# First tile projected without its shift, the shift's share added in PSUM, and later panels given a new split

## The chip, the cores and the metric

The kernel runs on one core of one Trainium2 chip. The metric is the device time of one execution in microseconds. Before the change the median of three runs is 1839.45 us (1839.06 to 1840.63).

A core has five engines that run their own instruction queues beside each other and wait for one another through semaphores: TensorE (PE) for matmuls, VectorE (DVE), ScalarE (ACT), GpSimd (POOL), and SyncE (SP), which here issues the transfers between device memory and the core's own memories. PE writes its results to PSUM, of which this kernel holds eight buffers (banks) of up to 128 x 512 fp32 numbers; DVE and ACT read them from there.

## The reference

Two layers over a sequence of 2048 frames of width 1024, each a normalised, conditioned input, a mixer and a gated residual, and a last normalisation:

```python
c_act = jax.nn.silu(c)
for i in range(DEPTH):
    cond = c_act @ ada_w[i] + ada_b[i]
    shift = cond[:, None, :D_MODEL]
    scale = cond[:, None, D_MODEL:2 * D_MODEL]
    gate = cond[:, None, 2 * D_MODEL:]
    h = rmsnorm(x, norm_g[i]) * (1.0 + scale) + shift
    ...
    x = x + gate * out
return rmsnorm(x, final_g)
```

Layer 0 is a recurrent block: `h @ in_w` gives 2 x 1024 columns, one half through a causal convolution of four taps, two gates and a linear recurrence over time, the other half as a SiLU gate, then an output projection. Layer 1 is a gated delta rule with eight heads of 128: `h @ in_w` gives q, k, v and z, 4 x 1024 columns, and 16 more columns, from which each head's decay and beta come. Everything is fp32.

What matters for the change: the projection of the first layer is `(x_norm * scale + shift) @ W`, which equals `(x_norm * scale) @ W + shift @ W`. The second term is one row, the same for all frames.

## The kernel before, in words

**Products.** An fp32 product of a weight panel (1024 x 128) and a tile of 512 frames is made of three reduced products (fp32r): both operands are split into a high and a low part, and high x high, high x low and low x high are summed in one PSUM bank. For each of 8 k-steps of 128 that makes three matmuls, 24 for a panel and a tile (`products`, line 721, matmul in line 728). Panels are loaded by `panel_load` (655) and split by `panels_thread` (665): `whi` on ACT (704), `wlo` on DVE (710). `keep_thread` (715) stores the low half for the second unit of frames.

**Order of work.** The program is written by a planner (`Weave`, lines 78 to 174) when it is built. Each thread is a generator; a `yield` names an event, a buffer slot, or an engine with the time that the step is thought to take there, and the planner picks the step that can start first (priority settles ties). This fixes the order of each engine's queue; on the chip only semaphores decide when things run. Durations of the steps off PE are scattered by one per cent by a random generator, so that its seeds choose among orders; before, `w.count()` sets a new seed of `SEEDS` every 16 jobs (88 to 91).

**Stages.** Layer 0 takes its frames in two units of 1024, each of two tiles of 512 (`in1`), with 16 panels, x and z in turn, then the output projection `out1`; layer 1 the same with 32 panels (`in2`), the heads beside it, and `out2`. A job is one panel and one tile (`job`, 731); `project_thread` (760) runs the jobs in the order of `plans` (639 to 651): in the first unit panels 0 and 1 over both tiles, these four jobs side by side, then the others one by one, each over both tiles.

**The start.** What must arrive is: the first tile of x, 2 MB (`norm_thread`, 526), the first panels, and the conditioning weights of layer 0, 4 MB each for scale and for shift, in four quarters of two k-steps (`first_loads_thread`, 330). SP issues x, panel 0, quarter 0 of scale and shift in turns, panel 1, quarters 1 and 2, the second tile of x, quarter 3. PE computes scale with four matmuls of 32 output columns side by side, each writing its own 32 partitions of one bank, called column groups here (396), sums these with `corner` (326, called from 403), and DVE finishes the columns (316, 319). DVE sums shift itself (422), and PE turns that into columns (427). Idle matmuls on the identity stand before and in between (380; `BEFORE`, `BEHIND`, line 38). The tile of x is scaled by its row norm (516), transposed by PE (550), and `split_thread` (614) makes `h = tile * scale + shift` on ACT (620), its high half on ACT or DVE (625, 628) and its low half on DVE (630). A k-step's products wait for that k-step's split.

**After a job.** `conv1_thread` convolves an x panel from PSUM (805 to 832, DVE line 819) and frees the bank; `z1_thread` makes the gate (846, 848). `gates_thread` makes the two gates (861), the recurrence (890) and the output. The banks: tags `mm`, `d`, `c` and `tp`, two each. The second unit's tiles are turned through device memory: `turned_thread` (575), scaled (516), transposed on DVE (563), stored, loaded again (`reload_thread`, 600) and split.

**The decay columns.** `decay_thread` (1062), once a unit, loads the 1024 x 16 weights, splits them into high and low side by side (32 columns), and for each tile runs 16 matmuls of 512 frames (1085) once all k-steps of the tile are split; then ACT copies, PE folds and turns (1096), and a chain on DVE and ACT makes decay and beta, on which all heads of the unit wait.

Of the kernel before, what the change touches and what calls it, by code (L numbers as in the profile page):

```python
# [17 lines left out]
P = 128  # L18
# [7 lines left out]
NH = 8  # L26
# [3 lines left out]
TP = 5  # L30
TURN = 2
# [6 lines left out]
BEFORE, BEHIND = (0, 3, 5, 0, 0, 0, 0, 0), (4, 0, 0, 0)  # L38
# [4 lines left out]
SEEDS, SPREAD = (32, 45, 51, 36, 4, 54, 53, 16, 3, 25, 36, 8, 28, 14, 37, 0, 0), 0.01  # L43
# [34 lines left out]
class Weave:  # L78
    def __init__(self):
        self.free = dict.fromkeys(("pe", "act", "dve", "pool", "sp", "dma"), 0.0)  # L80
        self.held = {"dve2": [], "pool2": []}
        self.table = "exp"
        self.landed, self.through = [0.0] * 8, 0.0
        self.scatter, self.jobs = random.Random(SEEDS[0]), 0
        self.threads = []
        self.now = 0.0

    def count(self):
        self.jobs += 1
        if self.jobs % 16 == 0:  # L90
            self.scatter = random.Random(SEEDS[self.jobs // 16])
# [86 lines left out]
def trunk_kernel(ctx, tc, x, head, small, ada0, ada_w, ada_b, final_g, w1, gate_w, ow1, w2, wab, ow2, out):  # L178
# [20 lines left out]
    def flat(ap):  # L199
# [13 lines left out]
    fold = cp.tile([32, 32], F32, name="fold")  # L213
    pool.memset(fold, 0.0)
    pool.tensor_tensor(fold[:, 0:16], ident[0:32, 0:16], ident[0:32, 16:32], ALU.add)

    corner = cp.tile([P, 1], F32, name="corner")
    dve.tensor_reduce(out=corner, in_=ident.rearrange("p (m c) -> p m c", c=32)[:, :, 0], axis=mybir.AxisListType.X,
                      op=ALU.add)

    small_s = cp.tile([P, SMALL], F32, name="small_s")

    def part_of(tile_in, at, *shape):
# [10 lines left out]
    cond = cp.tile([P, 2, 2, KT], F32, name="cond")  # L234
    sp2 = cp.tile([P, KT], F32, name="sp2")
# [11 lines left out]
    tags |= {t: ("l1", n) for t, n in {"xf1": 3, "tg": 4, "th": 2, "tz": 2, "gw": 2, "head": 1}.items()}  # L247
# [3 lines left out]
        "xe": 2, "xf": 2, "kt": KTN, "qt": QTN, "vt": 1, "ec": 4, "eca": 3, "gr": 1, "middle": 1, "ac": 4, "kd": 5, "vn": 4,  # L251
        "rq": 4, "nk": 4, "oo": 2, "tblk": 1, "ttmp": 1, "tf": 1, "zt": 2, "t2": 2, "yt": 2, "so": 2, "ro": 2,
        "ssk": 2, "ssq": 2, "rk": 2, "cc": 2, "junk": 1, "ab": 1, "gin": 1, "gg": 1, "spe": 1, "spd": 1, "beta": 2,
        "gs": 2, "eg": 2}.items()}

    for t in ("xe", "xf", "vt", "eca", "gr", "middle", "ab", "gin", "gg", "spe", "spd"):
        tags[t] = ("l2a", tags[t][1])
# [70 lines left out]
    H = TC // 2  # L328

    def first_loads_thread():  # L330

        yield ev("firstpanel")
        for q in range(4):
            if q == 1:
                yield ev("firstpanels")
            if q == 3:
                yield ev("loaded", (("in1", 0), 1))
            if q % 2 == 0:
                p = hp if q == 0 else pools["hc"]
                raws = [p.tile([P, KT, TC], F32, tag=f"h{'lh'[part]}{'BC'[q // 2]}", name=f"ada{part}{q}") for part in range(2)]  # L340
                raws = [flat(r).rearrange("p (a k c) -> p a k c", a=2, c=H) for r in raws]
            for part in range(2):
                w.set(ev("adaraw", part, q), raws[part][:, q % 2])
            for g in range(2):
                for part in (1, 0):
                    yield "sp", 1.3, False
                    sp.dma_start(out=raws[part][:, q % 2, 4 * g:4 * g + 4, :], in_=ada0[4 * part + q, :, 4 * g:4 * g + 4, :])
                    w.spawn(arrive_thread(ev("adaload", part, q, g)), 0)
            w.set(ev("adaissue", q))
# [28 lines left out]
    def idle_products(pt, n):  # L378
        for _ in range(n):
            pe.matmul(pt[:, 3 * P:4 * P], lhsT=ident, rhs=ident, start=True, stop=True)  # L380

    def first_pe_thread():

        rest = ps.tile([P, TC], F32, tag="mm", name="rest")
        idle_products(rest, 42)
        c_bc, ttok = yield ev("cbc")
        for q in range(4):
            raw = yield ev("adaraw", 1, q)
            ctok = yield slots["c"]
            pt = ps.tile([P, TC], F32, tag="c", name="adaps")  # L390
            for g in range(2):
                yield ev("adaload", 1, q, g)
                yield "pe", 1.15 if q + g else 2.2, 0.0 if g == 0 else 0.2
                idle_products(pt if g == 0 else rest, BEFORE[2 * q + g])
                for j in range(4):
                    pe.matmul(pt[32 * j:32 * j + 32, 0:H], lhsT=c_bc[:, 4 * g + j, :], rhs=raw[:, 4 * g + j, :],
# [4 lines left out]
            act.copy(tmp, pt[:, 0:H])  # L401
# [7 lines left out]
    def first_dve_thread():  # L409

        yield ev("c")
        for q in range(4):
# [10 lines left out]
            ctok = yield slots["c"]  # L423
            yield "pe", 0.5
            pt = ps.tile([P, TC], F32, tag="c", name="adac")
            idle_products(pt, BEHIND[q])
            columns_of(acc, pt, 2, ones[:, 0:1])
            put("tz", ttok)
            yield from finish_columns(0, 0, 2 * q, 2, pt[:, 0:2])
            put("c", ctok)  # L430
        yield ev("cond", 0, 1, KT - 1)
        w.set(ev("ada"))

# [92 lines left out]
    def norm_thread(key, layer, src, t0, slot, before, after, xtags=("b4",) * TB, htag="hf"):  # L526
# [17 lines left out]
        for k in range(KT):  # L544
            bank = "d" if slot == "A" and k % 2 else "tp"
# [29 lines left out]
    def turned_thread(key, layer, src, t0, slot, before, between, after):  # L575
# [16 lines left out]
        w.spawn(reload_thread(key, t_d), TP)  # L592
# [3 lines left out]
        for k in range(KT):  # L596
            xk, hold = yield ev("xk", key, k // 2)
            w.spawn(split_thread(layer, xk[:, k % 2, :], hold.done, hh, hl, k, ev("split", key, k), "hf"), 1)

    def reload_thread(key, t_d):  # L600
        for k in range(KT // 2):
# [4 lines left out]
            w.spawn(arrive_thread(ev("xk", key, k), (xk, Hold(w, slots["b4"], tok, 2))), 0)  # L606
# [6 lines left out]

    def split_thread(layer, pt, release_, hh, hl, k, done, tag, first=False):
        for part in (1, 0):
# [4 lines left out]
        act.activation(h, pt, AF.Identity, bias=cond[:, layer, 0, k:k + 1], scale=cond[:, layer, 1, k:k + 1])  # L620
# [1206 lines left out]
```

## Time and profile before

| | |
|---|---|
| median of 3 runs | 1839.45 us |
| the profiled execution | 1837.33 us |
| its span, first to last instruction | 1835.3 us |
| DVE busy | 1344.3 us |
| ACT busy | 1137.4 us |
| bytes moved | 322.76 MB, mean 176 GB/s |

The profile is of one execution. Its page gives busy time and share for each engine, the span in 40 slices, the DMA queues, the chain of work that ended last (followed back from the last instruction: at each step to what released it, or to the instruction before it on its engine), and the costliest groups of instructions. Further views used below: windows (busy time of each engine in a stretch), the order of time (start, length, engine, line, operation, output <- inputs, shapes, count, and in brackets idle time before and what ended it), the chain of waits in order of time, and groups by line. An fp32 matmul leaves two records (`x2`), an fp32r matmul one. Lengths of PE's records overlap, since matmuls are pipelined; the step from one to the next is shorter than the length.

### The profile page before, as it was taken

What the parts mean: (1) busy time and instruction counts of PE and PEld (TensorE: products, weight loads), DVE (VectorE), ACT (ScalarE), POOL (GpSimd) and SP (SyncE); (2) the same over time, 40 slices, a digit from 0 to 9 for tenths busy, and PEclk for the clock granted to TensorE, in tenths of its full rate; (3) what the DMA queues carried; (4) which work ended last, traced back from release to release, by engine and by line L of the source; (5) the groups of instructions that cost most, each with busy time, mean ns of one, the idle gap of its engine ahead of it and who ended that gap; (6) DMA issues with size and microseconds to landing.
All of it is one profiled execution on the core that took longest, in us unless ns stands there. A gap on an engine that the chain in (4) does not pass through costs nothing.

```text
span 1835.3 us, 31223 instructions
## 1 busy us (share of the span) xinstructions
PE 1806.3 (98%) x10378; PEld 1454.5 (79%) x10378; DVE 1344.3 (73%) x3113; ACT 1137.4 (62%) x2683; POOL 363.8 (20%) x895
## 2 busy tenths in 40 slices
PE   8999999999999999999999999999999999999998
PEld 7777777777877878787888788787888887878887
DVE  7989878777545647878788887677766786876653
ACT  5766777666112357687877676776787687664221
POOL 2111001000001014223333231231223132211100
PEclk9999999999999999999999999999999999999999
DMA  9567755555578735667677666456655556686741
GB/s 361 145 199 206 238 165 192 177 165 173 191 207 228 226 104 147 162 162 186 162 186 174 144 159 214 121 153 154 151 137 141 149 149 140 167 261 180 244 146 69
DMA packets 510425, 322.76 MB, mean 176 GB/s; under 512 B 369844, under 2 KB 437940, under 8 KB 510264
## 3 DMA queue, kind: packets, MB, share of 16 engines
q1 hardware_dynamic: 510264, 320.77, 62.7%
q8 instruction: 82, 1.34, 0.3%
q14 instruction: 79, 0.65, 0.1%
HBM read 219.93 MB, written 100.73 MB: 175 GB/s over the span
## 4 chain that ended last, share of the span: by engine, by line
PE 72%; DVE 10%; DMA 7%; ACT 5%; issue 2%; SPq 2%; POOL 1%; DVEq 0%; POOLq 0%; ACTq 0%
PE mm L728 41%; PE mmo L728 16%; PE pg L861 3%; DVE xf L781 2%; DMA raw<-in_w 1%; PE py L1454 1%; DVE tblk L1322 1%; PE pS L1467 1%; PE pS L1466 1%; PE pp L1437 1%; DVE ttmp L1319 1%; PE pp L1438 1%; PE pqk L1287 1%; PE pkk L1199 1%; DMA yf<-y_d 1%
## 5 line engine op out<-in xcount | busy, mean ns | idle before, releaser
L781 DVE SCALAR_TENSOR_TENSOR xf<-xe,small_s,xf 128x512 f32<-128x512 f32 x288 | 215.7, 753 | 49.8 <-ACT xf L1040 46.0
L704 ACT CAST whi<-raw 128x1024 fp32r<-128x1024 f32 x96 | 100.0, 1042 | 25.8 <-DMA raw<-in_w 20.6
L1319 DVE TENSOR_TENSOR ttmp<-blk,tblk 128x60 f32<-128x60 f32 (+24 forms) x496 | 104.7, 211 | 14.6 <-DMA blk<-blk_d 2.4
L1322 DVE TENSOR_TENSOR tblk<-tblk,ttmp 128x60 f32<-128x60 f32 (+24 forms) x496 | 105.7, 213 | 12.7 <-DVE ttmp L1319 0.3
L728 PE MATMUL mm<-hh_('in2', 1)_11643,whi 128*128 128x512 f32 x256 | 104.4, 408 | 0.6 <-ACT xe L793 0.5
L728 PE MATMUL mm<-hh_('in2', 1)_11918,whi 128*128 128x512 f32 x256 | 104.0, 406 | 0.7 <-ACT tz L1055 0.7
L728 PE MATMUL mm<-hl_('in2', 1)_11919,whi 128*128 128x512 f32 x256 | 104.0, 406 | 0.0
L728 PE MATMUL mm<-hh_('in2', 1)_11643,wlo 128*128 128x512 f32 x256 | 103.8, 405 | 0.0
L728 PE MATMUL mm<-hh_('in2', 0)_5199,whi 128*128 128x512 f32 x256 | 103.6, 405 | 0.0
L728 PE MATMUL mm<-hh_('in2', 1)_11918,wlo 128*128 128x512 f32 x256 | 103.5, 404 | 0.0
L728 PE MATMUL mm<-hl_('in2', 1)_11644,whi 128*128 128x512 f32 x256 | 103.5, 404 | 0.0
L728 PE MATMUL mm<-hh_('in2', 0)_5088,wlo 128*128 128x512 f32 x256 | 103.4, 404 | 0.0
L728 PE MATMUL mm<-hh_('in2', 0)_5088,whi 128*128 128x512 f32 x256 | 103.3, 404 | 0.0
L728 PE MATMUL mm<-hh_('in2', 0)_5199,wlo 128*128 128x512 f32 x256 | 103.2, 403 | 0.0
L728 PE MATMUL mmo<-oh,oh 128*128 128x512 f32 (+1 forms) x264 | 103.1, 390 | 0.0
L728 PE MATMUL mm<-hl_('in2', 0)_5200,whi 128*128 128x512 f32 x256 | 102.9, 402 | 0.0
L728 PE MATMUL mm<-hl_('in2', 0)_5089,whi 128*128 128x512 f32 x256 | 102.8, 402 | 0.0
L728 PE MATMUL mmo<-ol,oh 128*128 128x512 f32 (+1 forms) x264 | 102.5, 388 | 0.0
L728 PE MATMUL mmo<-oh,ol 128*128 128x512 f32 (+1 forms) x264 | 102.4, 388 | 0.0
L728 PE MATMUL mmo<-oh,yl 128*128 128x512 f32 x256 | 101.0, 395 | 1.1 <-DVE yl L971 1.1
L728 PE MATMUL mmo<-oh,yh 128*128 128x512 f32 x256 | 101.0, 395 | 0.4 <-ACT yh L967 0.4
L728 PE MATMUL mmo<-ol,yh 128*128 128x512 f32 x256 | 100.8, 394 | 0.0
(325 smaller groups left out, 5315.8 us busy)
## 6 DMA issues: line engine op xcount, KB each, us to landing
raw<-in_w SPq DMA_DIRECT2D x96, 512.0 KB, 4.1
araw<-in_ada_w SPq DMA_DIRECT2D x32, 512.0 KB, 4.7
xt<-x_d SPq DMA_DIRECT2D x32, 512.0 KB, 5.4
xt_d<-xb SPq DMA_DIRECT2D x192, 64.0 KB, 2.7
xk<-xt_d SPq DMA_DIRECT2D x24, 512.0 KB, 6.2
xt<-in_x SPq DMA_DIRECT2D x16, 512.0 KB, 6.3
ada<-in_ada SPq DMA_DIRECT2D x16, 512.0 KB, 10.9
y_d<-tz SPq DMA_DIRECT2D x32, 256.0 KB, 3.3
```

The lines of the kernel that those rows point to most:

```text
L704: act.copy(hi, raw)
L728: pe.matmul(pt, lhsT=lhs[a][:, k, :], rhs=rhs[b][:, k, :], start=(k == 0 and n == 0), stop=(k == KT - 1 and n == 2))
L781: dve.scalar_tensor_tensor(xf, xe[:, 1 + j:1 + j + TC], wc[:, j:j + 1], xf, ALU.mult, ALU.add)
L861: pe.matmul(pg, lhsT=gw[:, g, :], rhs=xf, start=True, stop=True)
L1199: pe.matmul(pkk[:, b, :], lhsT=kc, rhs=kc, start=True, stop=True)
L1287: pe.matmul(pqk[:, b, :], lhsT=kt[:, b * P:(b + 1) * P], rhs=qt[:, b * P:(b + 1) * P], start=True, stop=True)
L1319: dve.tensor_tensor(tmp, blk[:, j, j + 1:32].unsqueeze(2).to_broadcast([P, r, c_]), t[:, j, 0:c_].unsqueeze(1).to_broadcast([P, r, c_]), A ...
L1322: dve.tensor_tensor(t[:, j + 1:32, 0:c_], t[:, j + 1:32, 0:c_], tmp, ALU.subtract)
L1437: pe.matmul(pp[:, 0, :], lhsT=kc, rhs=S_, start=True, stop=True)
L1438: pe.matmul(pp[:, 1, :], lhsT=qc, rhs=S_, start=True, stop=True)
L1454: pe.matmul(py, lhsT=rm[:, b, :], rhs=zt, start=True, stop=True)
L1466: pe.matmul(pS[:, 0, :], lhsT=kd[:, b, :], rhs=yt, start=True, stop=True)
```

## The change

1. **Conditioning.** `first_loads_thread` loads all of scale, then all of shift; `first_panels_thread` loads four panels, one behind the first x tile and the others each behind a quarter of scale. The idle products between are gone.
2. **First tile without shift.** `split_thread` applies only the scale to the first tile. Jobs 0 to 3 are panels 0 to 3 on the first tile, jobs 4 to 7 the same panels on the second; all eight are spawned together. Panels 2 and 3 are split into buffers (`yh`, `yl`) that are used only later otherwise.
3. **The shift's share.** `bias_thread` multiplies the four panels with the shift as soon as that is there (16 matmuls for a panel, four column groups, fp32), splits the result, and two more products per panel add it to the bank through `comb`, in which each column sums the four groups.
4. **New split.** After jobs 0 to 3, `shift_thread` adds the shift to the first tile, k-step by k-step, and splits it again; from the fifth panel on jobs wait for that.
5. **Second tile.** Its x is loaded behind all of the shift, into the buffers of the first tile.
6. **Decay columns.** `ab_thread` runs them in fp32, four k-steps side by side in the four column groups, on h before its split; the weights are loaded once. In layer 1 `split_over_thread` makes h in place.
7. **Order.** One seed; `TP` 5 to 4, `TURN` 2 to 3 (transposed blocks in flight), three `tz` buffers for two.

```diff
-TP = 5
-TURN = 2
+TP = 4
+TURN = 3
...
-BEFORE, BEHIND = (0, 3, 5, 0, 0, 0, 0, 0), (4, 0, 0, 0)
...
-SEEDS, SPREAD = (32, 45, 51, 36, 4, 54, 53, 16, 3, 25, 36, 8, 28, 14, 37, 0, 0), 0.01
+SEED, SPREAD = 4, 0.01
...
+    FIRST = 4
...
     def first_loads_thread():
         yield ev("firstpanel")
...
+        for part in (1, 0):
...
+            for q in range(4):
+                w.set(ev("adaraw", part, q), raws[q // 2][:, q % 2])
+                for g in range(2):
+                    yield "sp", 1.3, False
+                    sp.dma_start(out=raws[q // 2][:, q % 2, 4 * g:4 * g + 4, :], in_=ada0[4 * part + q, :, 4 * g:4 * g + 4, :])
+                    w.spawn(arrive_thread(ev("adaload", part, q, g)), 0)
+                w.set(ev("adaissue", part, q))
+                if part and q == 0:
+                    yield ev("panelissue", q + 1)
+
+    def first_panels_thread():
+        name, panels, _ = plans[0]
+        yield ev("small")
+        yield ev("loaded", (("in1", 0), 0))
+        for m in range(FIRST):
+            if m:
+                yield ev("adaissue", 1, m - 1)
+            got = yield from panel_load(name, panels[m])
...
+    def bias_thread():
+        name, panels, jobs = plans[0]
+        ctok = yield slots["hf"]
+        yield ev("c")
+        yield "dve", 0.6
+        comb = tile_([P, TC], "hf", "comb", F32R)
+        dve.tensor_copy(out=comb, in_=corner.to_broadcast([P, TC]))
+        for k in range(KT):
+            yield ev("cond", 0, 0, k)
...
+        for n in range(FIRST):
+            halves = (yield ev("w", name, panels[n]))[0:2]
+            btok = yield slots["c"]
...
+            pt = ps.tile([P, P], F32, tag="c", name="pbias")
+            yield "pe", 0.55, 0.0
             for g in range(2):
...
+                for a in range(2):
+                    for j in range(4):
+                        pe.matmul(pt[32 * j:32 * j + 32], lhsT=sh[:, 4 * g + j, :], rhs=f(halves[a])[:, 4 * g + j, :],
+                                  start=(g + a == 0), stop=(g + a == 2))
+            yield "act", 0.3
+            act.copy(both[:, n % 2, 0, :], pt)
+            yield "dve", 0.25
+            dve.tensor_tensor(both[:, n % 2, 1, :], pt, f(both[:, n % 2, 0, :]), ALU.subtract)
...
+        for n in range(FIRST):
+            yield ev("job", name, n)
...
+            w.spawn(shift_thread(key, hh, hl, k), 2)
+
+    def shift_thread(key, hh, hl, k):
+        ttok = yield slots["hf"]
+        yield "act", 0.711
+        t = tile_([P, TC], "hf", "hs")
+        act.activation(t, f(hh[:, k, :]), AF.Identity, bias=cond[:, 0, 0, k:k + 1], scale=1.0)
+        yield "dve2", 0.599
+        dve.tensor_tensor(t, t, f(hl[:, k, :]), ALU.add)
+        yield "act", 0.524
+        act.copy(hh[:, k, :], t)
+        yield "dve2", 0.599
+        dve.tensor_tensor(hl[:, k, :], t, f(hh[:, k, :]), ALU.subtract)
...
     def split_thread(layer, pt, release_, hh, hl, k, done, tag, first=False):
-        for part in (1, 0):
+        for part in (1,) if first else (1, 0):
             yield ev("cond", layer, part, k)
...
+        if first:
+            act.activation(h, pt, AF.Copy, scale=cond[:, layer, 1, k:k + 1])
...
+        if u == 0:
+            jobs = [(p, i) for i in range(NTC) for p in panels[:FIRST]] + [(p, i) for p in panels[FIRST:-2] for i in range(NTC)] + pair(*panels[-2:])
...
     def job(name, jobs, n):
...
+        yield from products(pt, (hi, lo), h, (lambda k: ev("shifted" if first and n >= FIRST else "split", (name, i), k)),
+                            more=first and n < FIRST)
+        if first and n < FIRST:
+            comb, both = yield ev("bias", n)
+            for a in range(2):
+                yield "pe", MM, 0.0
+                pe.matmul(pt, lhsT=both[:, a, :], rhs=comb, start=False, stop=(a == 1))
...
+    def ab_thread(u):
+        yield ev("wab")
         for i in range(NTC):
...
+            for g in range(0, KT, 4):
+                hs = []
+                for k in range(g, g + 4):
+                    hs.append((yield ev("h", (("in2", u), i), k)))
...
+                yield "pe", 0.87, 0.0 if g == 0 else 0.2
+                for k in range(4):
+                    pe.matmul(pab[32 * k:32 * k + 32], lhsT=wab_s[:, 16 * (g + k):16 * (g + k) + 32], rhs=hs[k][0], start=(g == 0), stop=(g > 0))
...
-        w.spawn(norm_thread((in1[0], 1), 0, x, TC, "B", [ev("adaissue", 2)], [ev("cond", 0, 1, 3), ev("cond", 0, 0, 3)],
-                            ("yh", "yh", "yl", "yl"), "tg"), 2)
+        w.spawn(norm_thread((in1[0], 1), 0, x, TC, "B", [ev("adaissue", 0, 3)], [ev("cond", 0, 1, KT - 1)], htag="tg"), 2)
```

More of the change, by code (lines that the diff above doesn't have):

```diff
@@ L422, in first_dve_thread, with shift_columns_thread @@
                     dve.scalar_tensor_tensor(acc, raw[:, k], c_col[:, k:k + 1], acc, ALU.mult, ALU.add)
[L423 to L430, printed above, removed]
+            w.spawn(shift_columns_thread(q, acc, ttok), 0)
+        for k in range(KT):
+            yield ev("cond", 0, 0, k)
         yield ev("cond", 0, 1, KT - 1)
         w.set(ev("ada"))
+    def shift_columns_thread(q, acc, ttok):
+        ctok = yield slots["c"]
+        yield "pe", 0.4
+        pt = ps.tile([P, 2], F32, tag="c", name="adac")
+        columns_of(acc, pt, 2, ones[:, 0:1])
+        put("tz", ttok)
+        yield from finish_columns(0, 0, 2 * q, 2, pt)
+        put("c", ctok)
     def columns_thread():
@@ L544, in norm_thread @@
         for k in range(KT):
-            bank = "d" if slot == "A" and k % 2 else "tp"
+            bank = "tp"
             ptok = yield slots[bank]
@@ L741, in job @@
         bank = ("d" if layer == 1 else "c") if kind in "vz" else "mm"
-        if name == ("in1", 0) and n < 4:
-            bank = "mm" if n < 2 else "d"
+        first = name == ("in1", 0) and i == 0
         mtok = yield slots[bank]
         pt = ps.tile([P, TC], F32, tag=bank, name="mm")
-        yield from products(pt, (hi, lo), h, (lambda k: ev("split", (name, i), k)))
+        yield from products(pt, (hi, lo), h, (lambda k: ev("shifted" if first and n >= FIRST else "split", (name, i), k)),
[5 more added lines that the diff above has]
+                pe.matmul(pt, lhsT=both[:, a, :], rhs=comb, start=False, stop=(a == 1))
         if all(q != p for q, _ in jobs[n + 1:]):
-            put("whi", htok)
-            put("wlo", ltok)
+            put(*htok)
+            put(*ltok)
         if layer == 1:
@@ L765, in project_thread @@
             for n in range(len(jobs)):
-                w.count()
-                if name == ("in1", 0) and n < 4:
+                if name == ("in1", 0) and n < 2 * FIRST:
                     w.spawn(job(name, jobs, n), 8 + n)
-                    if n == 3:
-                        for m in range(4):
+                    if n == 2 * FIRST - 1:
+                        for m in range(2 * FIRST):
                             yield ev("job", name, m)
@@ L1747, in trunk_kernel @@
         w.spawn(xr_thread(), 3)
+        w.spawn(wab_thread(), 3)
+        for u in range(NU):
+            w.spawn(ab_thread(u), 2)
         w.spawn(phase1_end_thread(), 0)
```

195 lines of the change are left out of this document (104 added, 91 removed).

## The prediction

> **What bounds the kernel now.** I read the page first: the busy shares and the chain of work that ended last.
>
> ```profile
> PE 1806.3 (98%) x10378; PEld 1454.5 (79%) x10378; DVE 1344.3 (73%) x3113; ACT 1137.4 (62%) x2683; POOL 363.8 (20%) x895
> ...
> PE 72%; DVE 10%; DMA 7%; ACT 5%; issue 2%; SPq 2%; POOL 1%; DVEq 0%; POOLq 0%; ACTq 0%
> ```
>
> TensorE (PE) is busy nearly always and carries 72% of the chain. So an edit is worth what it takes from PE's work, or from the stretches in which PE has none. Next, the windows view, in four stretches (after the length: PE, weight loads, DVE, ACT, POOL).
>
> ```profile
> 0.00:56.00 56.00, 51.02 (x347) 40.82 (x347) 44.83 (x115) 30.14 (x51) 11.77 (x29) 1.00 0.76 296
> 100.00:1800.00 1700.00, 1682.74 (x9709) 1355.95 (x9709) 1246.55 (x2918) 1070.29 (x2571) 341.84 (x841) 1.00 0.64 174
> 45.00:105.00 60.00, 60.00 (x257) 46.08 (x256) 55.92 (x99) 41.53 (x63) 7.41 (x16) 1.00 0.51 141
> 660.00:670.00 10.00, 8.78 (x45) 6.98 (x45) 6.38 (x22) 5.92 (x11) 0.49 (x3) 1.00 0.01 2
> ```
>
> Between 100 and 1800 us PE idles only 1700 - 1682.7 = 17.3 us. The start looks busy too, 51.0 of 56, but the order of time on PE shows with what:
>
> ```profile
> 1.52 12.49 PE L380 MATMUL rest<-ident 128*128 128x128 f32 x84 [1.52 <-POOL ident masks.py:199]
> 13.95 0.64 PE L396 MATMUL adaps<-ada,c_bc 128*32 128x256 f32 x8
> ...
> 15.78 0.64 PE L396 MATMUL adaps<-ada,c_bc 128*32 128x256 f32 x8
> ...
> 21.70 1.32 PE L550 MATMUL tph<-ident,xt 128*128 128x128 f32 x8 [0.39 <-ACT h L620]
> ...
> 23.52 0.50 PE L728 MATMUL mm<-hh_('in1', 0)_265,whi 128*128 128x512 f32 x1
> ...
> 29.87 0.61 PE L326 MATMUL adaps<-corner,atmp 128*128 128x1 f32 x4 [0.28 <-ACT atmp L401]
> ...
> 35.23 0.64 PE L396 MATMUL adaps<-ada,c_bc 128*32 128x256 f32 x8 [1.05 <-DMA ada<-in_ada]
> ...
> 37.57 0.50 PE L728 MATMUL mm<-hl_('in1', 0)_266,whi 128*128 128x512 f32 x1 [0.57 <-DVE hl_('in1', 0)_266 L630]
> ...
> 38.46 0.64 PE L396 MATMUL adaps<-ada,c_bc 128*32 128x256 f32 x8
> ...
> 42.39 0.58 PE L326 MATMUL adac<-ones,acc 128*128 128x1 f32 x4 [1.10 <-DVE cond L319]
> ```
>
> Twelve microseconds are idle products on the identity; the first real product (mm) stands at 23.52. To price what PE did that has to be done anyway I take each kind's step from the chain of waits, where a piece ends as the next begins, and counts from the groups and from the windows of line 728 alone:
>
> ```profile
> 23.02 0.57 PE adaps L396 x8
> ...
> 24.71 0.34 PE adaps L326 x4
> ...
> 45.72 0.44 PE tph L550 x4
> ...
> 46.82 0.70 PE mm L728 x3
> ...
> 57.30 0.86 PE pg L861 x2
> ```
>
> ```profile
> L550 PE MATMUL tph<-ident,xt 128*128 128x128 f32 x64 | 9.7, 279 | 0.4 <-ACT h L620 0.4
> L396 PE MATMUL adaps<-ada,c_bc 128*32 128x256 f32 x64 | 5.1, 391 | 1.1 <-DMA ada<-in_ada 1.1
> ```
>
> ```profile
> 0.00:56.00 56.00, 22.15 (x78) 13.78 (x78) 1.00 0.76 296
> ```
>
> A product takes 0.70/3 = 0.23 us. By 56 us PE has done 78 x 0.23 = 17.9 of products, 64/4 x 0.44 = 7.0 of transposes, 64/8 x 0.57 = 4.6 of conditioning and some 8 x 0.34 = 2.7 of columns: 32.2 us. So 23.8 us of the start are lost. Up to 23.5 the useful work is 6 x 0.44 + 4 x 0.57 + 2 x 0.34 = 5.6, the loss 17.9; the other 5.9 come later, 3.0 of them as the waits of 0.28, 1.05, 0.57 and 1.10 above (the rest is change-over between kinds).
>
> **Part 1, the first product.** Before, each quarter of scale travels with its quarter of shift, and a k-step needs both. After, scale goes first, and shift needs no k-step. A 512 KB transfer takes 0.524 MB / 408 GB/s = 1.29 us at the rate of the row below, and the queue is full.
>
> ```profile
> 20.00:30.00 10.00, 9.27 (x75) 5.94 (x74) 8.61 (x21) 5.59 (x10) 0.00 (x0) 1.00 1.02 408
> ```
>
> The quarter that starts the work had its last scale piece eighth in the queue (four x blocks, a panel, then scale, shift, scale), used at 15.78. After the change it is seventh: 14.5. The last scale quarter was 25th, used at 38.46; it becomes 16th: 38.46 - 9 x 1.29 = 26.9. What follows an arrival shows in ACT's and DVE's rows:
>
> ```profile
> 16.48 0.37 ACT L401 COPY atmp<-adaps 128x256 f32<-128x256 f32 x1 [4.75 <-PE adaps L396]
> ...
> 18.12 0.16 DVE L319 SCALAR_TENSOR_TENSOR cond<-cond,head_s 128x2 f32<-128x2 f32 x1
> ...
> 20.86 1.45 ACT L620 ACTIVATE h<-tph,cond 128x512 f32<-128x512 f32 x2 [1.36 <-DVE cond L316]
> ...
> 22.20 1.13 ACT L625 CAST hh_('in1', 0)_265<-h 128x512 fp32r<-128x512 f32 x2
> 22.87 1.29 DVE L630 TENSOR_TENSOR hl_('in1', 0)_266<-h,hh_('in1', 0)_265 128x512 fp32r<-128x512 f32 x2
> ```
>
> From the conditioning matmul (15.78) to the end of the scale (18.28) are 2.5 us, from h (20.86) to the first product (23.52) 2.7. So the first product comes at 14.5 + 5.2 = 19.7, say 19.5, since the columns need not queue behind idle products. By then PE can have done 4 transposes, 4 conditioning groups and one pair of columns, 1.8 + 2.3 + 0.3 = 4.4; loss 15.1 instead of 17.9, **2.8 gained**. The next three quarters land 3.9 us apart (three transfers: two scale, one panel), and each opens 4 panels x 2 k x 3 = 24 products, 5.5 us. From some 22 us on PE has a backlog, and the 3.0 us of waits go: **3.0 gained**; what is late next is PE itself.
>
> Moved behind all shift pieces on SP's queue are the second tile's four x loads, from places 19 to 22 to places 25 to 28, 6 x 1.29 = 7.7 us later, about 41 us; they also wait for buffers that the first tile holds until its last split, about 31. With scaling and split, the second tile's products start near 47. Until then PE has the first tile's 96 products (22 us) with transposes, conditioning and columns (5 us), 19.5 + 27 = 46.5: covered, without slack. The stores of low halves and the next panel's load go later still, and nobody waits for them then.
>
> **Part 2, the share of the shift.** Added on PE, per panel: 16 matmuls of 128 columns in four column groups (the loops of bias_thread) and two full products. Four matmuls of width 256 in four groups took 0.57 above, where one alone would take half of pg's 0.86, 0.43: 0.14 over. Width 128 gives 0.22 + 0.14 = 0.36, four times 1.4 per panel. Ends: no surcharge 0.9, no overlap 16 x 0.22 = 3.4. I take 1.4, the nearest row: 4 x 1.4 + 8 x 0.23 = **7.4 lost** (5.4 to 15.4); PE is full by then, so nothing hides it. The wait that is added: these products close each bank behind the last shift column. DVE sums shift in steps of about 0.51:
>
> ```profile
> 38.88 2.56 DVE L422 SCALAR_TENSOR_TENSOR acc<-ada,c_col,acc 128x256 f32<-128x256 f32 x5
> ```
>
> The 24th transfer is usable at 37.2; four sums, columns and copies bring the share to some 42. Jobs of later panels stand behind it in PE's order; PE has other products until 46.5, a cover of 4 us.
>
> **Part 3, the new split.** For panels from the fifth on, the first tile gets its shift and is split again. The groups of DVE between 45 and 105 us:
>
> ```profile
> L563 DVE STREAM_TRANSPOSE xb<-xt 128x512 f32<-128x512 f32 x8 | 5.6, 700 | 0.0
> ...
> L630 DVE TENSOR_TENSOR hl_('in1', 0)_520<-h,hh_('in1', 0)_519 128x512 fp32r<-128x512 f32 x7 | 4.5, 679 | 0.0
> ...
> L516 DVE TENSOR_SCALAR xt<-xt,rs 128x1024 f32<-128x1024 f32 x4 | 3.0, 747 | 0.0
> ```
>
> That adds 8 x (1.45 + 1.13)/2 = 10 us on ACT (h and cast, rows above), which is 41.5 of 60 busy there, and 16 x 0.68 = 11 us on DVE, which has 60 - 55.9 = 4.1 free and can put off the preparation of the next tiles (lines 563 and 516). Cover: 4.1 + 5.6 + 3.0 = 12.7 against 11, so I cost it at nothing; without that cover it is up to 11 us.
>
> **Part 4, the decay columns (line 1085).** Four times 16 matmuls against split weights become eight groups of four fp32 matmuls in four column groups, on h before its split.
>
> ```profile
> 648.62 3.71 PE pab L1085 x16
> ```
>
> ```profile
> L1085 PE MATMUL pab<-hh_('in2', 1)_11918,wabh 128*32 128x512 f32 x8 | 3.2, 396 | 0.0
> ```
>
> Eight such groups of 8 make 64, or 4 x 3.7 = 14.8 us. After: 0.86 + 0.14 = 1.0 per group, 8.0 in all: **6.8 gained** (0.86 each: 7.9 gained; no overlap, 3.4 each: 12.7 lost). The Trainium skill, "TensorEngine Tiling (Array Packing)", Theoretical Speedup, allows up to 4x for outputs of at most 32 columns; by it four cost what one does and 7.9 are gained, where the row of 0.57 shows 1.72/0.57 = 3.0x. Since the columns no longer wait for the split, the decay chain starts earlier, and I count the idle 10 - 8.8 = **1.2 gained** at 660 (0 to 1.2).
>
> **The sum.** 2.8 + 3.0 - 7.4 + 6.8 + 1.2 = 6.4 us less. The profiled execution took 1837.33 (span 1835.3, 2.0 around it), 2.1 below the median of 1839.45; 1837.33 - 6.4 = 1830.9 there, **1833 against the median**. A measurement of this kernel can tell about 0.2%, 3.7 us: faster is below 1835.8, slower above 1843.1.
>
> **Rivals.** *DVE becomes the bound* (the slower one): between 45 and 105 the split's 11 us push back the operations that empty PSUM, and PE waits for banks. For it: 55.9 of 60 busy, and four panels end together. Against: the cover of 12.7. It decides once less than about 1 us of the 12.7 can be put off; whole price 11: 1844.
>
> *The order is drawn anew*: one seed for 17, so every DVE, ACT and POOL queue is reordered. The 17.3 us of idle are small waits. If they grow by two thirds, 11 us: 1844. Against: nothing in a seed adds work.
>
> *The start doesn't open early*, because casts of four panels and the scale chain share ACT: the 5.8 don't come, 1839, no change.
>
> *PE runs slow after a pause.* The removed idle products kept PE at work between 14 and 20. The windows of PE alone show the same matmul at two rates:
>
> ```profile
> 2.00:3.00 1.00, 1.00 (x7) 1.00 0.76 104
> ...
> 13.00:14.00 1.00, 1.00 (x14) 1.00 0.99 406
> ```
>
> Half rate lasted from about 2 to 7 us. If a sparse stretch brings it back for 5 us, 2.5 to 3 us are lost: 1836. The Trainium skill, "TensorE: Matmul & The Clock Gate", Why this matters for your kernels, warns of gaps above 3 us between bursts; by that rule the removal costs this, and the trace agrees on the half rate (7 against 14) though the profile's clock column says 1.00.
>
> *Column groups overlap fully*: 2.0 from the shift's share and 1.1 from the decay columns, 1830.
>
> **Chances.** Forecast 0.40 (1829 to 1836), full overlap 0.12, no early start 0.10, slow clock 0.06, DVE 0.16, order 0.16. Faster: 0.37 + 0.12 + 0.03 = 0.52. Same: 0.03 + 0.10 + 0.03 + 0.03 + 0.03 = 0.22. Slower: 0.13 + 0.13 = 0.26. The range, 1824 to 1846, holds all but the heavier half of the two slow rivals and a small rest below. The forecast's own range is 1829 to 1836.
>
> **What would show it.** Right: first mm near 19.5; no wait above 0.5 on PE between 22 and 60; pbias near 1.4 per panel and pab near 1.0 per group; no idle PE at 660. Wrong: PE waits for mm or d banks between 45 and 105 released by DVE; idle between 100 and 1800 well above 17; mm steps of 0.46 near 20.

## The result and the profile after

The kernel after takes 1856.41 us (median of five, 1855.3 to 1857.28) against 1839.45 before (five runs, 1837.76 to 1840.63): a ratio of 1.0096 with an interval of 1.0085 to 1.0108. It is slower by 1%, and outside the predicted range. The profiled execution took 1856.24, with a span of 1854.3 against 1835.3: 19.0 us to be found.

The page of the kernel after, busy times and chain, and the four stretches of the windows view (after the length: PE, weight loads, DVE, ACT, POOL, then granted clock, DMA share and GB/s):

```profile
PE 1816.5 (98%) x10486; PEld 1456.6 (79%) x10486; DVE 1348.1 (73%) x3131; ACT 1152.4 (62%) x2708; POOL 353.8 (19%) x894
...
PE 74%; DVE 9%; DMA 7%; ACT 6%; issue 2%; SPq 2%; POOL 1%; DVEq 0%; POOLq 0%; ACTq 0%
```

```profile
0.00:56.00 56.00, 51.39 (x389) 42.73 (x390) 39.97 (x103) 27.83 (x46) 9.99 (x27) 0.97 0.80 314
100.00:1800.00 1700.00, 1675.47 (x9644) 1343.23 (x9643) 1247.89 (x2927) 1081.36 (x2583) 334.95 (x844) 1.00 0.63 175
45.00:105.00 60.00, 58.05 (x362) 43.84 (x362) 52.21 (x101) 41.21 (x67) 4.74 (x10) 1.00 0.33 90
660.00:670.00 10.00, 10.00 (x49) 8.22 (x48) 5.83 (x8) 6.47 (x12) 1.12 (x4) 1.00 0.37 113
```

PE is busy for 10.2 us more (1816.5 against 1806.3) and idle for 8.8 more (37.8 against 29.0). Half of the loss is work that takes longer, half is waiting. Between 100 and 1800 the idle time is 24.5 us instead of 17.3; the hole at 660 is gone, as forecast.

The order of time on PE at the start, then one row of ACT, then the granted clock there (the share of full speed that the profile lists for PE; 0.50 is half clock. Windows of PE: length, busy, clock, DMA share, GB/s):

```profile
16.78 0.64 PE L457 MATMUL adaps<-ada1h,c_bc 128*32 128x256 f32 x8 [1.54 <-DMA ada1h<-in_ada]
18.96 0.64 PE L457 MATMUL adaps<-ada1h,c_bc 128*32 128x256 f32 x8 [1.54 <-DMA ada1h<-in_ada]
19.53 1.82 PE L615 MATMUL tph<-ident,xt 128*128 128x128 f32 x8
21.14 0.85 PE L319 MATMUL adaps<-fold,atmp 128*128 128x1 f32 x4
21.86 0.77 PE L813 MATMUL mm<-hh_('in1', 0)_266,whi 128*128 128x512 f32 x1
22.43 0.63 PE L813 MATMUL mm<-hl_('in1', 0)_267,whi 128*128 128x512 f32 x1
...
60.51 1.28 PE L836 MATMUL mm<-comb,bias 128*128 128x512 f32 x4
63.14 0.50 PE L813 MATMUL mm<-hh_('in1', 0)_606,whi 128*128 128x512 f32 x1 [1.36 <-DVE tz L937]
```

```profile
18.31 0.62 ACT L709 CAST hh_('in1', 0)_266<-h 128x512 fp32r<-128x512 f32 x1
```

```profile
18.00:20.00 2.00, 1.04 (x11) 0.93 1.02 416
20.00:22.00 2.00, 2.00 (x12) 0.50 1.03 420
22.00:24.00 2.00, 2.00 (x9) 0.72 1.02 418
```

The first product stands at 21.86, not at 19.5. Its high half is there at 18.93 (the row of ACT), but in PE's queue the second quarter's conditioning, transposes and columns stand ahead of it, and the last piece of that quarter is used at 18.96. The clock falls to half behind the two waits for transfers, and the first products follow each other by 0.57 us instead of 0.23. Before the second tile's first product (63.14) PE waits 1.36 us for VectorE to empty a bank. When the start is over, about 3 us are lost instead of gained: in its order of time the kernel before has 96 products and the start's other work done at 63.64, and 3.5 us of that are gate products (`pg`) which the kernel after still has to do.

The waits of PE between 60 and 1800 us, after and before (in all, times, longest):

```profile
PE pk L1256 <- ACT kt L1143: 4.5, 1, 4.5
PE pqk L1378 <- ACT qt L1143: 4.5, 5, 2.6
```

```profile
PE pg L861 <- DVE tg L879: 1.8, 1, 1.8
PE pp L1437 <- DVE state L1480: 1.7, 2, 1.0
```

The longest wait before is 1.8 us; after there is one of 4.54, at 1420, in a stage that the change hardly touches. What follows it:

```profile
1420.57 1.12 PE L1256 MATMUL pk<-ident,kt 128*128 128x128 f32 x4 [4.54 <-ACT kt L1143]
```

```profile
1421.00:1423.00 2.00, 2.00 (x8) 0.50 0.79 268
1423.00:1425.00 2.00, 2.00 (x6) 0.50 0.02 4
1425.00:1427.00 2.00, 2.00 (x53) 0.75 0.00 0
1427.00:1429.00 2.00, 2.00 (x10) 1.00 0.00 0
```

The wait is paid twice: PE stands for 4.5 us and then works at half clock for 5.4 us, until 1426.0, which costs another 2.7.

Last, the step of the products. Two rows each, 18 products apart and with nothing between but such products, of before and of after:

```profile
1209.01 0.39 PE L728 MATMUL mm<-hl_('in2', 1)_11919,whi 128*128 128x512 f32 x1
...
1213.09 0.39 PE L728 MATMUL mm<-hl_('in2', 1)_11644,whi 128*128 128x512 f32 x1
```

```profile
1211.79 0.40 PE L813 MATMUL mm<-hh_('in2', 1)_11806,wlo 128*128 128x512 f32 x1
...
1215.95 0.40 PE L813 MATMUL mm<-hh_('in2', 1)_12070,wlo 128*128 128x512 f32 x1
```

18 steps take 4.08 us before and 4.16 after, both at full clock. Over all products that follow one another directly between 70 and 1600 us (some 3,400 steps in each trace) the mean step is 0.2290 before and 0.2315 after. A page of the profile doesn't show this; it is 1.1% of the work of both input projections; the products of out1 step by 0.230 in both kernels. There are 24 products in each of the 192 jobs of these projections, so 4608 x 0.0025 = 11.5 us.

### The profile page after: what moved, and what is told of

Read it like the earlier page. It is cut to its first block, busy times and chain, and to the rows that moved or that the text cites. A ratio compares the mean times of both kernels' runs of the same rounds, so it can differ in the third digit from the quotient of the medians.

```text
span 1854.3 us, 31457 instructions
## 1 busy us (share of the span) xinstructions
PE 1816.5 (98%) x10486; PEld 1456.6 (79%) x10486; DVE 1348.1 (73%) x3131; ACT 1152.4 (62%) x2708; POOL 353.8 (19%) x894
## 3 DMA queue, kind: packets, MB, share of 16 engines
q8 instruction: 83, 1.36, 0.3%
## 4 chain that ended last, share of the span: by engine, by line
PE 74%; DVE 9%; DMA 7%; ACT 6%; issue 2%; SPq 2%; POOL 1%; DVEq 0%; POOLq 0%; ACTq 0%
PE mm L813 42%; PE mmo L813 19%; DMA raw<-in_w 3%; PE pg L950 3%; DVE xf L870 2%; DVE tblk L1413 1%; DVE ttmp L1410 1%; PE pqk L1378 1%; PE pkk L1290 1%; PE pS L1557 1%; PE pp L1528 1%; PE py L1545 1%; PE pS L1558 1%; PE pp L1529 1%; DMA oraw<-in_ow 1%
## 5 line engine op out<-in xcount | busy, mean ns | idle before, releaser
L1413 DVE TENSOR_TENSOR tblk<-tblk,ttmp 128x60 f32<-128x60 f32 (+24 forms) x496 | 107.0, 216 | 12.8
L813 PE MATMUL mm<-hh_('in2', 1)_11806,whi 128*128 128x512 f32 x256 | 104.8, 409 | 1.4 <-ACT tz L1151 1.4
L813 PE MATMUL mm<-hh_('in2', 1)_12070,wlo 128*128 128x512 f32 x256 | 105.7, 413 | 0.0
L813 PE MATMUL mm<-hl_('in2', 1)_12071,whi 128*128 128x512 f32 x256 | 105.4, 412 | 0.0
L813 PE MATMUL mm<-hl_('in2', 0)_5332,whi 128*128 128x512 f32 x256 | 105.2, 411 | 0.0
L813 PE MATMUL mm<-hh_('in2', 0)_5196,wlo 128*128 128x512 f32 x256 | 104.7, 409 | 0.0
L813 PE MATMUL mm<-hh_('in2', 1)_11806,wlo 128*128 128x512 f32 x256 | 104.4, 408 | 0.0
L813 PE MATMUL mm<-hh_('in2', 0)_5331,wlo 128*128 128x512 f32 x256 | 104.3, 407 | 0.0
L813 PE MATMUL mm<-hh_('in2', 1)_12070,whi 128*128 128x512 f32 x256 | 104.1, 407 | 0.0
L813 PE MATMUL mm<-hh_('in2', 0)_5331,whi 128*128 128x512 f32 x256 | 103.8, 405 | 0.0
L813 PE MATMUL mm<-hl_('in2', 0)_5197,whi 128*128 128x512 f32 x256 | 103.6, 405 | 0.0
```

The costliest lines, as they stand in the source:

```text
L813: pe.matmul(pt, lhsT=lhs[a][:, k, :], rhs=rhs[b][:, k, :], start=(k == 0 and n == 0), stop=(k == KT - 1 and n == 2 and not more))
L1413: dve.tensor_tensor(t[:, j + 1:32, 0:c_], t[:, j + 1:32, 0:c_], tmp, ALU.subtract)
```

## The experiments

The theories as they arose. **A**: the order of work. The kernel before changes its random seed 16 times, with a list of 17 seeds; the change has one seed, so every queue is drawn anew, and the list's order is lost. **B**: the change's own parts cost the time. **C**: a sum of a slower start, decay columns that save 7 us, and an order worth plus or minus 10. **D**: the decay columns cost time. **P**, which came last: the products' step, through the places of tiles in SBUF. Every ratio is to the kernel before on the same chip. No run changes `TP`, `TURN` or the third `tz` buffer alone, so these stay untested.

### The order alone

Edit to the kernel before (number 4, 33, 1, 40, 13 or 19), and the calls of `count` gone; and the change with another number:

```diff
-SEEDS, SPREAD = (32, 45, 51, 36, 4, 54, 53, 16, 3, 25, 36, 8, 28, 14, 37, 0, 0), 0.01
+SEED, SPREAD = 4, 0.01
```

> The kernel before with one seed, 4, for the whole program instead of 17; nothing else is changed. Theory A (the seventeen seeds of before held an order that fits the chip, and the change lost that order): 1850 us, between 1845 and 1858, with more small waits of PE between 640 and 1650 us. Theory B (the parts of the change cost the time: the share of the shift, the second split, held banks and buffers, other counts of blocks in flight): 1839 us, at most 4 away.

> The kernel before with one seed, 33. Theory A: again 1845 to 1858, and some us away from the run with seed 4. Theory B: 1839, at most 4 away.

> The kernel before with one seed, 1. Theory A: again 1845 to 1858. Theory B: 1839, at most 4 away.

> The changed kernel with seed 33 for seed 4. Theory A: it moves by several us against 1856.4, to anywhere between 1845 and 1862, since only the order differs. Theory B: 1856, at most 4 away.

> The whole change with seed 42, whose order the planner rates best of 64. Theory C: out1 starts 6 to 9 us later than 452, as in both runs of the change so far; the time is 1836 to 1842, some 7 above the kernels with the decay columns alone.

> The kernel before with one seed (13) for the whole order, nothing else. Theory A (the order alone moves 20 us; 17 seeds had been chosen together and hold an order that few single seeds reach): between 1840 and 1865, as the three single seeds so far (1845, 1858, 1865), and no faster than 1839. Rival (single seeds are as good as the list, those three were unlucky): 1832 to 1839.

Measured: b_one4 1.0042 (1.0025 to 1.0058), b_one33 1.0144 (1.0123 to 1.0165), b_one1 1.0111 (1.0090 to 1.0132), b_one13 1.0009 (0.9999 to 1.0019); the change with seed 33 1.0011 (0.9997 to 1.0025), with 42 1.0029 (1.0018 to 1.0040). With b_one40 and b_one19 (below) the kernel before moves by 30 us with nothing but the seed (1835 to 1865), the change by 15 (1841 to 1856). That the order matters is shown. How it costs time the traces tell. In the table, idle is PE's idle time from in2's first product to the last stage's, as the windows view gives it, for instance for before, after and b_one33 (two stages each):

```profile
634.90:1131.50 496.60, 490.14 (x3233) 1.00 0.65 163
1131.50:1637.90 506.40, 499.39 (x3441) 1.00 0.60 152
```

```profile
644.80:1146.00 501.20, 488.39 (x3237) 1.00 0.64 164
1146.00:1653.10 507.10, 497.44 (x3353) 0.99 0.57 147
```

```profile
634.70:1136.40 501.70, 489.87 (x3209) 0.99 0.63 158
1136.40:1665.70 529.30, 512.29 (x3482) 0.99 0.58 147
```

and clock is the time lost at half clock from 60 to 1800, the sum of (1 - granted clock) x 20 over windows of 20 us; up to 0.7 us of it falls into the waits and is counted twice. Both are of the profiled execution, the ratio is of the medians; for b_one13 the profiled execution took 1844.14, its median is 1839.18.

| kernel | idle, us | clock, us | both | ratio |
|---|---|---|---|---|
| before | 13.5 | 0 | 13.5 | 1 |
| b_one40 | 13.0 | 1.8 | 14.8 | 0.9988 |
| b_one13 | 16.1 | 3.6 | 19.7 | 1.0009 |
| b_one4 | 17.2 | 5.2 | 22.4 | 1.0042 |
| b_one19 | 25.4 | 8.6 | 34.0 | 1.0107 |
| b_one1 | 27.0 | 7.0 | 34.0 | 1.0111 |
| b_one33 | 28.8 | 8.8 | 37.6 | 1.0144 |
| after | 22.5 | 5.0 | 27.5 | 1.0096 |
| change, seed 33 | 11.7 | 1.8 | 13.5 | 1.0011 |
| change, seed 42 | 12.8 | 0 | 12.8 | 1.0029 |

Within the kernel before, "both" accounts for the ratio: from before to b_one33 it grows by 24 us, and the time by 26. So a seed does its harm by a few long waits of PE in in2, and by the half clock that comes with them. After against the change with seed 42: 14.7 more in "both", 14.6 in the median (12 by the ratios). The change with seeds 33 and 42 has no more in "both" than before and is yet a little slower, with 42 clear of noise; half clock before 60 (3.4 and 5.1 us lost) and the products' step, below, are what it has besides.

### The decay columns

The parts of the diff that touch `split_over_thread`, `wab_thread`, `ab_thread` and the tables that they use, put into the kernel before with one seed; each kernel has a partner with that seed above or below.

```diff
-            for k in range(KT):
-                for q in range(2):
-                    pe.matmul(pab, lhsT=whl[:, k, :], rhs=hpr[q][:, k, :], ...
+                for k in range(4):
+                    pe.matmul(pab[32 * k:32 * k + 32], lhsT=wab_s[:, 16 * (g + k):16 * (g + k) + 32], rhs=hs[k][0], ...
```

> The kernel before with one seed, 4, and of the change only the decay columns (fp32, four column groups, on h before its split, weights loaded once). Theory C (the change is a sum of three: a start that loses 6 to 9 us by the first product of out1, decay columns that save about 7 us of PE work, and an order that moves the time by up to 10 us either way): out1 starts at 452, as with seed 4 alone, and the time is 1845.3 - 7 = 1838, with 6 us either way for the order. Theory D (the decay columns cost time, by holding a bank and buffers longer): over 1846.

> The same with seed 40, another order that the planner rates well. Theory C: out1 near 452, 1830 to 1840. Theory D: over 1842.

> The same with seed 19, whose order the planner rates best of 64. Theory C: out1 starts near 452; the time is below 1838, about 1833, since neither the start's loss nor a bad order is in it. Theory D: over 1842.

> The kernel before with one seed (40) for the whole order, nothing else: the pair of the run that has the decay columns as well and the same seed (1836.96). Theory C (decay columns save 5 to 7 us of TensorE's work, whatever the order): 1842 to 1844, in2's two stages together 5 to 7 longer than that run's 996.1, out1's stage 4 to 5 shorter than its 187.5, and the rest alike. Theory D (the columns save nothing): 1837 give or take 2. Theory A adds that the order after layer 0 is drawn anew by any change, by plus or minus 10, so only the two stages' work on TensorE (busy time), not their length, is the clean reading.

> The kernel before with one seed (19), nothing else: the partner of the run that has the decay columns as well (1830.3, 0.9960 of before). If the columns are worth their 7 us of TensorE's work: 1835 to 1839 (0.999 to 1.002 of before), TensorE's idle time in out1's and in2's stages alike in both. If TensorE only waits longer instead, as in the pairs with seeds 4 and 40: 1827 to 1832, its busy time in those stages 6 to 7 us higher and its idle time as much lower.

Measured, without and with the columns: seed 4 1.0042 and 1.0075 (1.0057 to 1.0094), a miss of 13 us for theory C; seed 40 0.9988 (0.9977 to 1.0) and 0.9992 (0.9982 to 1.0002); seed 19 1.0107 (1.0076 to 1.0138) and 0.9960 (0.9944 to 0.9976). The sign changes with the seed, so the columns' worth in time isn't settled; b_one19 (1857.87) lies 19 us and more above both of its expectations. What becomes of their work on PE the pair with seed 40 shows, whose stages begin within 8 us of each other: one window over out1's and in2's stages, b_one40 and then h_one40, and h_one40's longest waits:

```profile
455.00:1640.00 1185.00, 1171.94 (x7511) 1.00 0.64 167
```

```profile
455.00:1640.00 1185.00, 1165.17 (x7472) 1.00 0.63 166
```

```profile
PE pk L1176 <- ACT kt L1063: 6.3, 5, 1.6
PE pS L1477 <- ACT yt L1471: 2.3, 3, 1.3
```

The two windows are of one length, so that PE is busy for 6.8 us less says only that it idles for 6.8 more. The work follows from the same stages by their own ends, out1's first product to out2's first: busy 1171.4 and 1163.7 us, of which 1.7 are half clock that only b_one40 has. That is some 6 us less to do (with seeds 4 and 19, reckoned alike, 2.6 and 5.0; without half clock the mean is 1170.0 over the seven orders without the columns and 1163.6 over the three with them), and the stretch is only 0.9 shorter, since PE idles for 19.8 us instead of 13.1. Most of that is for ScalarE's tile `kt` (6.3 us here, 0.8 in b_one40; with seeds 4 and 19 these waits grow too, from 3.3 to 4.5 and from 1.2 to 3.5). In these stages PE is 98 to 99% busy and yet not the only bound. h_one19, 1830.29 us, is the fastest version of all and beats both kernels.

### The start

Two kernels from the change with seed 42 (1841.81), with every engine's order of work unchanged. a_warm42 fills PE's gaps ahead of the scale's products with products of the identity; a_nobias42 leaves the share of the shift out.

```diff
+    IDLE = (0, 2, 6, 7, 0, 0, 0, 0)
...
+                idle_products(pt if g == 0 else rest, IDLE[2 * q + g])
```

> The change with one seed of the order (42), and 15 products of the identity that fill TensorE's gaps ahead of the second, third and fourth group of the columns' products, as the kernel before has them; every engine's order of work is otherwise that of the change with seed 42 (1841.81 us; granted clock 0.61 at 18:19, 0.50 from 19 to 28, 0.77 at 28:29; out1's first product at 460.0). Nothing is left out. Theory C (the start loses by its parts, one of them the clock): clock 1.00 from 18 to 29, steps of 0.23 at once, out1's first product 2 to 4 us earlier (456 to 458), total 1838.5 to 1840. Rival (VectorE's and ScalarE's halves set the pace of the first products, so a faster TensorE only waits): the clock is full, but out1's first product stays at 459.5 to 460.5 and the total at 1841 to 1842.5, with new waits for halves between 23 and 63.

> The change with seed 42 and, on every engine, its order of work, but without the shift's share of the first four panels: the 64 narrow products, the eight products that add the share, and the four copies and four subtractions of the shares are left out (so the first tile's first four panels lack the shift). Theory C (the share's 5.9 us of TensorE's work stand in the path): out1's first product at 453 to 455, total 1835 to 1837. Rival (VectorE's late halves set the start, the share runs beside them): out1's first product at 458.5 to 460, total 1840 to 1842, the gaps before the second tile's products growing by as much as the share took.

Measured: 1.0031 (1.0018 to 1.0045) and 1.0040 (1.0026 to 1.0054), against 1.0029 for the kernel they are made from: the 2 to 7 us that theory C expected did not come; both medians lie 2 to 3 us above what the rivals expected, too. The clock between 20 and 26 us, first without and then with the idle products, is mended:

```profile
20.00:26.00 6.00, 6.00 (x33) 0.50 1.03 421
```

```profile
20.00:26.00 6.00, 6.00 (x50) 1.00 1.02 416
```

The second tile's first product, in the order seed 42, idle products, no share:

```profile
66.29 0.50 PE L813 MATMUL mm<-hh_('in1', 0)_604,whi 128*128 128x512 f32 x1 [1.35 <-DVE tz L937]
```

```profile
62.98 0.60 PE L816 MATMUL mm<-hh_('in1', 0)_619,whi 128*128 128x512 f32 x1 [1.35 <-DVE tz L940]
```

```profile
63.48 0.80 PE L805 MATMUL mm<-hh_('in1', 0)_604,whi 128*128 128x512 f32 x1 [5.35 <-DVE tz L928]
```

With the share left out, PE is done some 7 us earlier (58.1 for 64.9) and waits 5.35 us for VectorE, which sums the shift, splits the second tile and only then empties the first bank (`tz`); half clock follows until 67.1. The second tile starts 2.8 us earlier, and out1's first product comes 1.4 earlier (458.6 for 460.0), not the 5 to 7 that were expected. So two chains of about the same length end at 63 to 66, PE's and VectorE's; cutting one shows the other. The idle products gained 3.3 us by 63, but the clock fell to half behind the wait of 1.35, and out1's first product came 0.7 earlier (459.3 for 460.0).

### The places of the tiles

Why do products step by 0.2315 in every kernel with the new start, and by 0.2290 in every one without? In the built programs the two halves of the panels lie elsewhere: the new threads ask for tiles in another order, and the places of a pool's tags are given out in the order of first asking. Before (and with the decay columns alone) the low half's two buffers are followed directly by the high half's; in the change the tags `hf`, `tt` and `rs` lie between. The edit asks for all tags once, ahead of everything; all five kernels use it, with the orders of tags that their expectations name; every engine's order of work is that of the kernel that each is made from:

```diff
+    for t, n in (("b4", 2 * TC), ("raw", 2 * TC), ("ss", KT), ("tt", TC), ("rs", 1), ("wlo", 2 * TC), ("whi", 2 * TC), ("ed", 12), ("hf", TC)):
+        for _ in range(tags[t][1]):
+            tile_([P, n], t, "place")
```

> The change with seed 42, every engine's order of work unchanged, only the places of the tiles in SBUF as in the kernel before: the panels' high half follows the low half's two buffers at once (low at 119,168, high at 127,360; in the change low at 114,944, high at 131,456). Nothing is left out. Theory P (the places make each product's step 0.2316 us instead of 0.2290): step 0.229, total 1841.8 less 11.5 us, 1828 to 1833; out1's first product some 4 us earlier (456), in2's two stages 3 to 4 us shorter each. Theory A (only the order of work matters, the step is a by-product of something else): step 0.2316, 1840 to 1844.

> The change itself (its own seed, 4), same order of work, only the tags' places as in the kernel before. Nothing is left out. Theory P: step 0.229, total 1856.4 less 11.5, 1843 to 1847, which is where the kernel before with that seed stands (1845.3): then the places are 11 of the change's 19 us, the single seed in place of seventeen the other 8, and the change's own work about nothing. Theory A: 1854 to 1858.

> The kernel before with the change's decay columns and one seed (19), which took 1830.3, same order of work, only the tags' places as in the change (low half at 114,944, high half at 131,456). Nothing is left out. Theory P: step up from 0.229 to 0.2316, total 1840 to 1844. Theory A: 1829 to 1832.

> The change with seed 42, same order of work, the tags of the panels' halves as far apart as in the change (16,512 bytes) but both below byte 131,072 (low at 90,240, high at 106,752), the transposed tiles and raw panels moved up behind them. Nothing is left out. Theory P with the boundary as its cause: step 0.229, 1828 to 1833. Theory P with the distance as its cause: step 0.2316, 1840 to 1844. A step between, or above 0.2316, would say that it is neither alone, but where these tiles lie against those that other engines use.

> The change with seed 42, same order of work, the panels' low half at the change's address (114,944), the high half right behind it (123,136), the tags that stood between them moved behind both. Nothing is left out. Distance theory: step 0.229, total as with the kernel before's places (1836.9), 1834 to 1840. Address theory (the low half's place decides, or which tags lie around it): step 0.2316 to 0.233, 1840 to 1845.

| kernel | places | mean step, us | ratio | made from, ratio |
|---|---|---|---|---|
| a_place42 | as before | 0.2291 | 0.9989 (0.9978 to 1.0) | seed 42, 1.0029 |
| a_place4 | as before | 0.2291 | 1.0085 (1.0067 to 1.0102) | after, 1.0096 |
| h_place19 | as the change | 0.2315 | 0.9986 (0.9976 to 0.9996) | h_one19, 0.9960 |
| a_low42 | apart, both below byte 131,072 | 0.2327 | 1.0045 (1.0029 to 1.0060) | seed 42, 1.0029 |
| a_next42 | side by side at the change's address | 0.2320 | 1.0045 (1.0028 to 1.0062) | seed 42, 1.0029 |

The same 18 steps in a_place42, 4.08 us again:

```profile
1209.14 0.39 PE L817 MATMUL mm<-hl_('in2', 1)_11986,whi 128*128 128x512 f32 x1
...
1213.22 0.39 PE L817 MATMUL mm<-hl_('in2', 1)_11986,whi 128*128 128x512 f32 x1
```

That the places set the step is shown, in both directions. Of the 11.5 us that theory P expected, 7.4 came with seed 42 (0.40%), 4.8 with h_one19 the other way, and 2 with the change's own seed, which its interval doesn't tell from nothing. There, in the profiled execution, PE idles for 43.2 us instead of 37.9 and works at half clock for more of its time (10.8 us lost while it is busy, 6.1 in after): at 1099 it now stands for ScalarE's `qt` 4.36 us, in after 2.57, and the hole at 1422 is as it was.

```profile
1099.14 1.65 PE L1382 MATMUL pqk<-qt,kt 128*128 128x128 f32 x6 [4.36 <-ACT qt L1147]
```

Neither the byte 131,072 nor the distance of the halves is the cause by itself: a_low42 and a_next42 both keep the longer step. Which neighbours make it stays open.

## Why the prediction was wrong, point by point

**The order is drawn anew** is the rival that came true; it was given 0.16 and 11 us. The step that failed is its rebuttal, "nothing in a seed adds work". A seed adds long waits, and the half clock that comes with them adds 1.7 to 3.4 us each. With seed 4 the kernel before loses 0.42%, some 8 us; the 12 to 15 us that lie between the change's seeds 4 and 42 are in PE's idle time and its clock.

**A product of 0.23 us in both kernels** was taken without a word. The step went from 0.2290 to 0.2315: 11.5 us of PE's work, of which 2 to 7 reach the time.

**Part 1** (5.8 gained) failed. The first product came at 21.9 instead of 19.5. Only 0.7 of that is the half clock at 20 us: a_warm42 and a_place42 have full clock there, and their first products stand at 21.18 and 21.14. The rest is PE's queue. The first quarter's last piece was used by 13.4, earlier than the forecast 14.5, but VectorE finished its columns only behind the low half of a panel (15.57 to 16.80), and then the second quarter's work stood ahead of the product. The rival that named the clock was right on the place and asked 2.5 to 3 us; 1.7 were lost here, none to 5.1 in the other kernels of the change. The later waits of the start did go, but the side-by-side panels hold all four banks until the share is added, and VectorE, with the shift's sums ending near 50 instead of the 42 assumed, empties them late. The second tile starts at 63 to 66, against a forecast of full cover. With the places mended and no half clock (a_place42), out1's first product stands at 454.2, against 453.1 before: the start as such loses about 1 us. Parts 1 and 2 together were forecast to lose 1.6; that this comes near is luck, since neither came as it was worked out.

**Part 2** (7.4 lost) was near in size and wrong in place: the share takes 4 x 1.0 + 8 x 0.23 = 5.9 us (a panel's four groups from 52.89 to 53.91), and leaving it out did not shorten the run, since VectorE ends nearly as late.

```profile
52.89 0.42 PE L380 MATMUL pbias<-whi,sh 128*32 128x128 f32 x8
...
53.57 0.40 PE L380 MATMUL pbias<-wlo,sh 128*32 128x128 f32 x8
53.91 1.09 PE L615 MATMUL tph<-ident,xt 128*128 128x128 f32 x8
```

**Part 3** at nothing held to within 0.6 us. Between 45 and 105 PE is busy for 58.05 of 60 us and has two longer waits for banks that VectorE empties, as the DVE rival said, but not its 11 us: 1.36 at 63, before the new split begins on VectorE (67.2), so that this one belongs to part 1, and 0.59 at 97.

**Part 4** was right as work: 0.99 per group in the chain of waits of after (four products of 0.86 one after another would be 3.44), 7.9 us for eight groups in place of 14.8. As time it was not: with seed 40 PE waits for ScalarE instead, and with the other seeds the order outweighs it.

```profile
623.01 0.99 PE pab L1170 x8
```

**The 19.0 us.** Idle 8.8. Of the 10.2 us more of busy time the rows name: longer steps 11.5, the share 5.9, half clock while PE works 1.7 at the start and 4.4 later, less 6.9 for the decay columns and 4.1 for 14 idle products fewer (15.4 against 11.3 from row to row); that is 12.5, and some 2 us the other way lie in change-overs that the rows don't separate. By out1's first product after is 5.8 us behind (458.9 against 453.1), of which the steps of 1,536 products are 3.8 and the half clock 1.7. By experiments, the ratios of the single seed (1.0042), the decay columns on top (1.0075) and the rest of the change (1.0096) stand one after another for seed 4; each step redraws the order, so the shares are not the parts' own. At the best seed tried (of six for the kernel before, three with the decay columns, three for the change, two with the old places), the kernel before takes 0.9988, with the decay columns 0.9960, the change with the old places 0.9989, with its own 1.0011. As far as so few seeds can tell, what is left of the change without the order and the places is about nothing, where 6.4 us gained were forecast.

## What to carry to other kernels

Where a fixed order has been picked from many draws, an edit loses the draw: compare both versions over several orders, and look first at PE's longest waits and the clock behind them. An engine that is 98% busy need not be the bound: in the pair with seed 40 some 6 us of its work went and came back as waits, most of them for an engine that is 61% busy. After an edit that creates tiles in another order, compare the step between back-to-back matmuls of the two traces; if it moved, restore the places.

## What the runs showed of the hardware

**The clock.** In the 20 traces, between 60 and 1800 us, each of the 14 waits of PE above 2.3 us came with half clock, which began during the wait or just behind it and lasted 3.41 or 6.83 us (1.7 or 3.4 us lost); of those between 1.0 and 2.3 us most did not (2.25 did in a_low42, 2.28 did not in a_one33), and the wait of 1.36 at 63 did in some runs and not in others. The Trainium skill, "TensorE: Matmul & The Clock Gate", What's actually happening, has the rate change after an idle or a busy window of about 3.4 us, with windows that run freely; the 3.41 and 6.83 us agree with it. Its section HAM oscillation — how this bites in real kernels names gaps above some 3.4 us; here the measurement decides: 2.3 us were enough, and at the start of after two of 1.54 us close together, where 0.65 and 1.96 us in a_place42 were not.

**The places.** The same matmul on the same shapes steps by 0.2290, 0.2315, 0.2320 or 0.2327 us with the place of its operands in SBUF, at full clock and in both input projections; the products of out1 step by 0.230 us in all 20 traces.
